# Block sums taken out of PSUM at the transposes, eps inside the sums of squares, and two gate tiles as a pair of seven half products

## The chip, the core and the metric

The kernel runs on one core of a Trainium2 chip. The core has a matrix engine (TensorE, PE in the profile; its weight loads are PEld), a vector engine (VectorE, DVE), a scalar engine (ScalarE, ACT), a general one (GpSimd, POOL), and a queue that only issues transfers (SyncE, SP). Each engine works through its own list of instructions in order, and engines wait for each other by semaphores. TensorE writes only to PSUM, eight banks of 128 x 512 float32; the other operands lie in SBUF. The metric is the device time of one execution in microseconds (us), less is better.

## What is computed

One decoder layer on x of 1024 tokens by 1024 channels, in float32:

```python
h = rms_norm(x, norm_w)                     # x * rsqrt(mean(x*x) + eps) * w, eps = 1e-5
proj = h @ w_in                             # 1024 x 7440
(a_q, a_k, a_v, a_gate, b_q, b_k, b_v, b_gate, b_low, m_a, m_b) = split(proj)
o_a = sliding_window_attention(rope(a_q), rope(a_k), a_v, sinks) * silu(a_gate)
log_a = log_sigmoid(b_low @ b_gate_up + bias) / 16
o_b = rms_norm(gated_linear_attention(b_q, b_k, b_v, log_a)) * silu(b_gate)
merged = sigmoid(m_a) * (o_a @ w_a_proj) + sigmoid(m_b) * (o_b @ w_b_proj)
return rms_norm(x + merged @ w_out, final_norm_w)
```

Attention has 16 query and 2 key heads of 64 with a window of 128; the linear attention has 4 heads with keys of 128 and values of 256. `m_a` and `m_b` are the two merge gates, 1024 columns each, that is eight tiles of 128 columns.

## The kernel before

**Products.** Every float32 operand of a large product is split into a high part (rounded to the type fp32r) and a low rest, and a product is three passes: high by high, high by low, low by high. `half_product` (L129) issues them for half of the 1024 channels: four slices of 128 channels, three matmuls each, of 128 x 128 weights by 512 tokens. `proj` (L137) joins two half products to one tile of 128 columns by 512 tokens.

**Token tiles.** At the start, eight tiles of 128 tokens are loaded and normalized by `token_tile` (L192). ScalarE squares a tile and sums it, GpSimd turns the sum into the reciprocal root by `rstd_of` (L144: mean plus eps, then power -0.5), VectorE multiplies by it and by the norm's weight `nwb`, which a transfer has copied to all partitions (L185, L198). TensorE transposes the tile into two PSUM banks, four blocks in each; ScalarE copies the high part out (L206) and VectorE subtracts for the low part (L207). These parts are `hT[th][i]`: `th` is the half of the tokens (tiles 0 to 3 or 4 to 7), `i` the half of the channels. The four blocks are called `b11`, `b21` (first tokens) and `b12`, `b22` (second tokens).

**Seven products.** Most columns of `w_in` are done two tiles at a time by `pair` (L567), which calls `seven_products` (L425): of the 2 x 2 blocks of weights and the 2 x 2 blocks of `hT` it makes seven half products instead of eight, as in Strassen's and Winograd's schemes. For this it needs four sums of blocks on the token side, `t1` to `t4`, each split into high and low. `t_sums` (L241) computes them from the split parts in SBUF: per slice of 128 channels ten sums on VectorE (L251, L252, L253, L258, L259), four copies on ScalarE (L245), four subtractions (L246). The order of the products in a pair is 1, 2 (with `b11`, `b21`), 6 (`t4`), 3 (`t2`), 5 (`t3`), 4 (`t1`), 7 (`b22`).

**Order of the stages.** First the token tiles; between them and behind them the first three tiles of the gate `m_a`, one half of the tokens at a time (`m_half`, L209). Then `t_sums`; the small product `low` (L329); tile 3 of `m_a` (`m_tiles([3])`, L348). Then the pairs: four of `m_b`, each followed by two calls of `log_gate`, with the rotary tables (`rotary_tables`, L353: some 30 small VectorE operations and two sines) behind the second; then pairs of `b_q`, `b_k`, `b_gate`, `b_v`. Then attention: in pass `i` of a loop `attend` (L717) works on one pair of heads while `prep` (L787) makes the queries and gates of the next. In the last pass there is nothing to prepare, and two tiles of `m_a` (4 and 5, from the list `fillers`) stand in its place. Then `gla(0)`, the linear attention of two heads, with tiles 6 and 7 of `m_a` spread over its steps by the list `pace`. Then the other two heads, with products of `w_a_proj` spread over them, and the merge, `w_out` and the final norm. There `finish` (L1075) sums four partial sums of squares, calls `rstd_of`, and scales and stores a token tile.

**What sets the order.** The program is written in one order, but a planner with a time line of its own puts each engine's instructions in line: where an engine would be free, it takes the earliest written instruction that it believes ready. Memory is taken from pools; a tile in a pool waits until the tiles that lay there before are released. The splits of weights (`split_w`, L116) run on ScalarE and on the engine in `rest[0]`, GpSimd at first.

Of the kernel before, what the change touches and what calls it, by code (L numbers as in the profile page):

```python
# [25 lines left out]
P = 128  # L26
# [43 lines left out]
def layer_kernel(ctx: ExitStack, tc: tile.TileContext, consts, x, positions, norm_w, w_in, a_sinks,  # L70
# [73 lines left out]
    def rstd_of(pool, ss, n, width):  # L144
        r = pool.tile([P, width], F32, name="rstd")
        nc.gpsimd.tensor_scalar(r, ss, 1.0 / n, EPS, ALU.mult, ALU.add)  # L146
        nc.gpsimd.tensor_tensor(r, r, mhalf[:, :width], ALU.pow)
        return r
# [21 lines left out]
    mhalf = const.tile([P, 8], F32, name="mhalf")  # L170
    nc.gpsimd.memset(mhalf, -0.5)
    c1 = ExitStack()
    c1.enter_context(banks(sc=2, pt=2, av=2))
    with ExitStack() as cx:
        xp = cx.enter_context(pool_of(name="xp", bufs=3, side="right"))
        xp1 = cx.enter_context(pool_of(name="xp1", bufs=1, side="right"))
        nwb = xp1.tile([P, D], F32, name="nwb")
        xts = [xp1.tile([P, D], F32, name=f"xt{t}") for t in range(NT)]

        def load(t):  # L180
            nc.sync.dma_start(xts[t], x[t * P : (t + 1) * P, :])
# [3 lines left out]
        nc.sync.dma_start(nwb, norm_w.to_broadcast([P, D]))  # L185
        load(1)
        w_first = [wtile(w_in, O_MA)]
        load(2)
        load(3)
        w_first.append(wtile(w_in, O_MA + P))  # L190

        def token_tile(t):  # L192
            xt = xts[t]
            junk = xp.tile([P, D], F32, name="junk", bufs=1)
            ss = xp.tile([P, 1], F32, name="ss")
            nc.scalar.activation(junk, xt, AF.Square, accum_out=ss)
            r = rstd_of(xp, ss, D, 1)
            nc.vector.scalar_tensor_tensor(xt, xt, r, nwb, ALU.mult, ALU.mult)  # L198
            for half in range(2):
                p = bank("sc" if half else "pt")  # L200
# [4 lines left out]
                hs, ls = (y[:, :, t % 4 * P : t % 4 * P + P] for y in hT[t // 4][half])  # L205
                nc.scalar.copy(hs, pv)  # L206
                nc.vector.tensor_sub(ls, pv, hs.bitcast(F32))  # L207

        def m_half(c, w, th, tag="pj"):  # L209
            p = bank(tag)  # L210
            for i in range(2):
                half_product(p, w[i], hT[th][i], i == 0, i == 1)
# [4 lines left out]
        for t in range(4):  # L217
            token_tile(t)
        for t in range(4, NT):
            load(t)  # L220
        w_first.append(wtile(w_in, O_MA + 2 * P))
        for t in range(4, NT):
            if t < 7:
                m_half(t - 4, w_first[t - 4], 0)
            token_tile(t)


    lp = gctx.enter_context(pool_of(name="lp", bufs=1, side="right"))
    rctx = ExitStack()
    rp = rctx.enter_context(pool_of(name="rp", bufs=1, side="right"))  # L230
    sctx = ExitStack()
    tp = sctx.enter_context(pool_of(name="tp", bufs=1))
# [913 lines left out]
```

## Time and profile before

| | us |
|---|---|
| median of 3 runs | 1078.42 (1078.25 to 1078.5) |
| the profiled execution | 1075.87 |
| its span, from first to last instruction | 1074.1 |
| TensorE busy | 1021.3 |
| VectorE busy | 766.1 |
| ScalarE busy | 544.8 |
| GpSimd busy | 520.4 |

The span is what the profile shows; the execution's own time is 1.8 us longer. A page of the profile gives busy times, the chain of work that ended last, and groups of instructions by the line that issued them. A row of such a group reads: line, engine, operation, output and input, shapes, how many; then busy time and the mean of one in ns; then the idle time of the engine before them and what ended it. A row of a time line has the start, the duration, the engine, the line and operation, and in brackets the idle time before it. The records of matmuls overlap, since TensorE begins one before the last has drained, so the time that a series of them takes is read from the starts.

### The profile page before, as it was taken

How to read it: one execution, taken by the hardware profiler on the slowest of the kernel's cores; microseconds unless marked ns; L12 is line 12 of the kernel's file. 1: busy time of each engine (PE TensorE's matmuls, PEld its weight loads, DVE VectorE, ACT ScalarE, POOL GpSimd, SP SyncE). 2: the span in 40 equal slices, each digit the busy share in tenths (PEclk: the TensorE clock that was granted, in tenths of full speed). 3: DMA queues.
4: the chain of work that ended last, by engine and by line, in shares of the span. 5: the costliest groups of instructions: out<-in, count | busy, mean ns of one | idle time of the engine just before them, and what ended most of it. 6: DMA issues, size and time to landing. Idle time of an engine off the chain costs nothing.

```text
span 1074.1 us, 16183 instructions
## 1 busy us (share of the span) xinstructions
PE 1021.3 (95%) x5544; PEld 867.9 (81%) x5544; DVE 766.1 (71%) x1318; ACT 544.8 (51%) x1320; POOL 520.4 (48%) x441
## 2 busy tenths in 40 slices
PE   4999999989999999999999999989999999997996
PEld 3786787867889998887888888878778887786996
DVE  5999877544765333369978887777856388899786
ACT  6345865333343123366766667647645244244455
POOL 6123555678897443755678676747843100000002
PEclk9999999989999999999999999999999999999999
DMA  8242444444233317221222222429775388443415
GB/s 264 72 135 69 138 147 139 155 138 135 102 110 108 117 40 216 60 60 55 74 60 60 79 70 79 137 85 297 245 224 159 109 274 256 131 145 99 158 60 196
DMA packets 126402, 141.06 MB, mean 131 GB/s; under 512 B 10352, under 2 KB 87024, under 8 KB 126320
## 3 DMA queue, kind: packets, MB, share of 16 engines
q1 hardware_dynamic: 126320, 140.03, 41.7%
q8 instruction: 44, 0.72, 0.3%
q14 instruction: 38, 0.31, 0.1%
HBM read 95.04 MB, written 40.24 MB: 126 GB/s over the span
## 4 chain that ended last, share of the span: by engine, by line
PE 55%; DVE 9%; POOL 5%; issue 4%; ACT 3%; DMA 2%; SPq 0%; POOLq 0%; DVEq 0%; ACTq 0%
PE pj L134 20%; PE sj L422 14%; PE sj L134 13%; PE av L773 2%; PE sc L733 2%; PE av L817 1%; DVE b L946 1%; DMA oraw<-sp_oa 1%; POOL q L651 1%; PE pt L757 1%; ACT sm L748 1%; POOL q L650 1%; PE sc L817 1%; DVE qb L714 1%; POOL cl L767 1%
## 5 line engine op out<-in xcount | busy, mean ns | idle before, releaser
L134 PE MATMUL pj<-o,wh 128*128 128x512 f32 x1088 | 354.5, 400 | 2.0 <-ACT o L206 1.9
L134 PEld LDWEIGHTS pj<-o,wh 128*128 128x128 f32 x1088 | 202.0, 190 | 43.7 <-ACT o L206 2.1
L134 PE MATMUL pj<-o,wl 128*128 128x512 f32 x544 | 216.4, 398 | 0.0
L118 POOL TENSOR_TENSOR wl<-sraw,wh 128x512 fp32r<-128x512 f32 (+1 forms) x98 | 157.8, 1627 | 110.4 <-ACT wh L117 105.3
L134 PEld LDWEIGHTS pj<-o,wl 128*128 128x128 f32 x544 | 102.8, 189 | 21.4
L134 PE MATMUL sj<-o,wh 128*128 128x512 f32 x352 | 111.1, 395 | 1.9 <-DVE o L459 1.0
L117 ACT CAST wh<-wr 128x1024 fp32r<-128x1024 f32 (+1 forms) x76 | 66.4, 890 | 77.6 <-PE sj L422 21.9
L146 POOL TENSOR_SCALAR rstd<-zs 128x1 f32<-128x1 f32 x8 | 2.7, 335 | 209.3 <-DVE zs L1078 208.8
L117 ACT CAST wh<-sraw 128x512 fp32r<-128x512 f32 (+1 forms) x98 | 63.4, 677 | 74.5 <-PE sj L134 20.8
L118 POOL TENSOR_TENSOR wl<-wr,wh 128x1024 fp32r<-128x1024 f32 x29 | 71.3, 2460 | 46.7 <-ACT wh L117 43.5
L134 PEld LDWEIGHTS sj<-o,wh 128*128 128x128 f32 x352 | 65.7, 187 | 18.4 <-ACT u L485 1.4
L476 DVE TENSOR_TENSOR u<-u,sj 128x512 f32<-128x512 f32 x48 | 32.9, 685 | 61.5 <-PE sj L422 32.7
L134 PE MATMUL sj<-o,wl 128*128 128x512 f32 x176 | 69.4, 394 | 0.0
L422 PE MATMUL sj<-wh,b 128*128 128x256 f32 x320 | 60.0, 289 | 7.0 <-DVE b L946 4.2
L422 PEld LDWEIGHTS sj<-wh,b 128*128 128x128 f32 x320 | 51.2, 197 | 7.7 <-DVE b L946 4.4
L422 PE MATMUL sj<-wh,o 128*128 128x256 f32 x320 | 55.8, 277 | 0.6 <-DVE o L539 0.6
L765 POOL TENSOR_TENSOR ch<-ph,cst 128x512 fp32r<-128x512 f32 x32 | 37.3, 1164 | 39.2 <-ACT ph L764 34.5
L748 ACT ACTIVATE sm<-sc,nm 128x129 f32<-128x129 f32 x128 | 45.7, 369 | 20.2 <-DVE nm L744 19.8
L134 PE MATMUL sj<-b,wh 128*128 128x512 f32 x160 | 49.2, 392 | 0.5 <-ACT wh L117 0.5
L459 DVE TENSOR_TENSOR c<-u,sj 128x512 f32<-128x512 f32 x48 | 32.7, 681 | 23.4 <-PE sj L422 6.4
L422 PEld LDWEIGHTS sj<-wh,o 128*128 128x128 f32 x320 | 48.7, 188 | 0.9 <-DVE o L539 0.8
L118 DVE TENSOR_TENSOR wl<-wr,wh 128x512 fp32r<-128x512 f32 (+1 forms) x47 | 41.6, 902 | 10.5 <-ACT wh L117 10.3
(313 smaller groups left out, 2706.7 us busy)
## 6 DMA issues: line engine op xcount, KB each, us to landing
sraw<-in_w_in_dram SPq DMA_DIRECT2D x32, 512.0 KB, 4.0
wr<-in_w_in_dram SPq DMA_DIRECT2D x26, 512.0 KB, 3.9
r<-sp_ob SPq DMA_DIRECT2D x28, 256.0 KB, 3.9
qs<-q SPq DMA_DIRECT2D x72, 64.0 KB, 2.0
xt<-in_x_dram SPq DMA_DIRECT2D x8, 512.0 KB, 8.5
sp_ma<-gt SPq DMA_DIRECT2D x16, 256.0 KB, 2.1
sp_mb<-c SPq DMA_DIRECT2D x16, 256.0 KB, 2.0
gt<-sp_cum SPq DMA_DIRECT2D x16, 256.0 KB, 3.5
```

Of the source, the lines that this page charges most:

```text
L117: nc.scalar.copy(h, raw)
L118: rest[0].tensor_sub(l, raw, h.bitcast(F32))
L134: nc.tensor.matmul(p, a[:, k, :], b[:, k, :], start=start and k == 0 and y == 0, skip_group_check=True, stop=stop and k == 3 and y == 2)
L422: nc.tensor.matmul(p, m[i][:, k, t * P : t * P + P], w[j][:, k, :], start=start and k == 0 and y == 0, skip_group_check=True, stop=stop an ...
L459: nc.vector.tensor_add(o, like(u[i][b], o), like(x[j][b], o))
L476: nc.vector.tensor_add(o[b], u[i][b], x[j][b])
L650: eng.tensor_mul(q, q, cos[:, sl])
L733: nc.tensor.matmul(s[:, h * 256 : h * 256 + 256], lq, kk[kv][x][:, k0 : k0 + 2, :].rearrange("p n t -> p (n t)"), start=x == 0, stop=x == 1)
L748: nc.scalar.activation(sm[:, j, :], sel[j // 2][:, j % 2, :], AF.Exp, bias=nm[:, j : j + 1], accum_out=den[:, j : j + 1])
L765: nc.gpsimd.tensor_mul(ch, ph.bitcast(F32), leb)
L773: nc.tensor.matmul(av[:, b * 256 : b * 256 + 256], val[:, blk, kv, :], part[:, 2 * b : 2 * b + 2, :], start=y == 0, stop=y == len(terms) - 1)
L817: nc.tensor.matmul(p, a[i], b[j], start=start and y == 0, stop=stop and y == 2)
```

## The change

1. **eps inside the sums of squares.** The token tiles get one more column that holds (eps x 1024)^0.5, and the squares are scaled by 1/1024, so that ScalarE's sum already is the mean plus eps. At the end the partial sums get a fifth column of eps. `rstd_of` becomes `power`, one GpSimd operation.
2. **The norm's weight** is loaded as one row; two matmuls with a row of ones bring it to all partitions, in two PSUM banks. The normalization becomes two operations per tile, one per half, each with its own transposes behind it.
3. **The block sums** are formed in `token_tile` for tiles 4 to 7, out of the PSUM banks of the transposes: six VectorE operations and one ScalarE copy per tile write the unsplit sums `tr`. Behind the first three gate tiles `t_split` splits them in the order `t4`, `t2`, `t3`, `t1`, with four copies and four subtractions each.
4. **Order of the start.** The first gate tile's first half is made in two parts of 256 tokens, the first after two token tiles (`m_part`). The splits of the first three weights run on VectorE. The rotary tables wait for the scan in the fourth `log_gate`.
5. **Gate tiles.** Tile 3 is no longer made at the start. Tiles 6 and 7 become a pair of seven products, behind the pairs of `m_b`. Tile 3 alone stands in the last pass of attention, tiles 4 and 5 in `gla(0)`.
6. **The end.** In `finish` the scaling of the last quarter goes from VectorE to GpSimd.

```diff
+    def power(pool, ss):
+        r = pool.tile([P, 1], F32, name="rstd")
+        nc.gpsimd.tensor_tensor(r, ss, mhalf, ALU.pow)
         return r
...
+        nwr = xp1.tile([1, D], F32, name="nwr")
+        ones = xp1.tile([1, P], F32, name="ones")
+        nc.vector.memset(ones, 1.0)
+        nc.scalar.activation(ones[:, :1], ones[:, :1], AF.Tanh)
+        nc.vector.memset(ones[:, :1], 1.0)
+        xts = [xp1.tile([P, D + 1], F32, name=f"xt{t}") for t in range(NT)]
+        for xt in xts:
+            nc.gpsimd.memset(xt[:, D:], (EPS * D) ** 0.5)
...
-        nc.sync.dma_start(nwb, norm_w.to_broadcast([P, D]))
+        nc.sync.dma_start(nwr, norm_w)
         load(1)
+        rest[0] = nc.vector
         w_first = [wtile(w_in, O_MA)]
         load(2)
         load(3)
-        w_first.append(wtile(w_in, O_MA + P))
+        nwb = [bank("av") for i in range(2)]
+        for i in range(2):
+            nc.tensor.matmul(nwb[i], ones, nwr[:, i * 512 : i * 512 + 512], start=True, stop=True)
...
-            nc.scalar.activation(junk, xt, AF.Square, accum_out=ss)
-            r = rstd_of(xp, ss, D, 1)
-            nc.vector.scalar_tensor_tensor(xt, xt, r, nwb, ALU.mult, ALU.mult)
+            nc.scalar.activation(junk, xt, AF.Square, scale=D**-0.5, accum_out=ss)
+            r = power(xp, ss)
             for half in range(2):
+                xh = xt[:, half * 512 : half * 512 + 512]
+                nc.vector.scalar_tensor_tensor(xh, xh, r, nwb[half], ALU.mult, ALU.mult)
                 p = bank("sc" if half else "pt")
...
+            if t >= 4:
+                r1, r2, r3, r4 = (y[:, :, sl] for y in tr)
+                (b11h, b11l), (b21h, b21l) = ([y[:, :, sl].bitcast(F32) for y in m] for m in hT[0])
+                nc.vector.tensor_sub(r1, ps[0], b11h)
+                nc.vector.tensor_sub(r1, r1, b11l)
+                nc.vector.tensor_sub(r2, ps[1], r1)
+                nc.scalar.copy(r3, ps[0])
+                nc.vector.tensor_sub(r3, ps[1], r3)
+                nc.vector.tensor_sub(r4, b21h, r2)
+                nc.vector.tensor_add(r4, r4, b21l)
...
+        token_tile(0)
+        token_tile(1)
+        p = bank("pj")
+        m_part(p, w_first[0], 0)
+        w_first.append(wtile(w_in, O_MA + P))
+        load(4)
+        w_first.append(wtile(w_in, O_MA + 2 * P))
+        for t in range(5, NT):
+            load(t)
+        rest[0] = nc.gpsimd
+        token_tile(2)
+        token_tile(3)
+        m_part(p, w_first[0], 1)
+        m_half(0, None, 0, p)
...
+    def t_split(i, tag):
+        m = [tph.tile([P, 4, 512], F32R, name=f"t{i}h"), slot(tpl if tag else tph, tag or "tl")]
+        r = tr[i - 1]
+        for k in range(4):
+            nc.scalar.copy(m[0][:, k, :], r[:, k, :])
+            nc.vector.tensor_sub(m[1][:, k, :], r[:, k, :], f(m, 0, k))
+        return m
...
-    fillers = list(range(4, 8))
+    fillers = [3, 4, 5]
...
-    t_sums()
+    t4, t2, t3, t1 = (t_split(*y) for y in ((4, None), (2, "t4"), (3, "t2"), (1, "t3")))
...
-    m_tiles([3])
...
         if c == 2:
-            rotary_tables()
+            with tc.issue_after(scan):
+                rotary_tables()
+    pair(O_MA + 6 * P, P, keep(sp_ma, 6 * P, "tanh"))
...
-                for _ in range(2):
-                    m_tiles([fillers.pop(0)])
+                m_tiles([fillers.pop(0)])
...
+    ssq = zw.tile([P, NT, 5], F32, name="ssq", bufs=1)
+    nc.gpsimd.memset(ssq[:, :, 4], EPS)
...
-        r = rstd_of(zw, ss, D, 1)
+        r = power(zw, ss)
...
-        nc.vector.tensor_scalar_mul(z1[:, o : o + 256], z1[:, o : o + 256], r)
+        nc.gpsimd.tensor_scalar_mul(z1[:, o : o + 256], z1[:, o : o + 256], r)
```

`m_part(p, w, q)` issues the same 24 products as `m_half`, but for 256 tokens each.

More of the change, by code (lines that the diff above doesn't have):

```diff
@@ L169, in layer_kernel @@
     le = cst[:, C_LE : C_LE + P]
[L170 removed]
+    mhalf = const.tile([P, 1], F32, name="mhalf")
     nc.gpsimd.memset(mhalf, -0.5)
+    sctx = ExitStack()
+    tpl = sctx.enter_context(pool_of(name="tpl", bufs=1))
+    sr = sctx.enter_context(pool_of(name="sr", bufs=4))
+    lp = gctx.enter_context(pool_of(name="lp", bufs=1, side="right"))
+    tctx = ExitStack()
+    td = tctx.enter_context(pool_of(name="td", bufs=1, side="right"))
+    tr = [slot(td if i == 1 else tpl, f"t{i}", F32) for i in range(1, 5)]
     c1 = ExitStack()
```

76 lines of the change are left out of this document (26 added, 50 removed).

## The prediction

> **What bounds the kernel now.** I read the page first: the share of each engine, then the chain that ended last, then tables of busy time by stretch for the start.
>
> ```profile
> PE 1021.3 (95%) x5544; PEld 867.9 (81%) x5544; DVE 766.1 (71%) x1318; ACT 544.8 (51%) x1320; POOL 520.4 (48%) x441
> ...
> PE 55%; DVE 9%; POOL 5%; issue 4%; ACT 3%; DMA 2%; SPq 0%; POOLq 0%; DVEq 0%; ACTq 0%
> ...
> 0.00:23.35 23.35, 8.56 (x37) 7.05 (x37) 11.86 (x13) 15.65 (x27) 13.04 (x20) 1.00 0.94 301
> 20.00:40.00 20.00, 19.33 (x88) 15.80 (x89) 19.29 (x36) 8.67 (x15) 8.81 (x9) 1.00 0.35 104
> 90.00:100.00 10.00, 7.80 (x33) 5.58 (x32) 9.73 (x13) 3.91 (x7) 2.99 (x2) 1.00 0.20 54
> 110.00:140.00 30.00, 29.05 (x126) 23.20 (x125) 25.77 (x33) 25.03 (x38) 17.11 (x12) 1.00 0.46 154
> 668.00:713.00 45.00, 44.10 (x246) 37.40 (x245) 37.22 (x72) 28.12 (x92) 31.15 (x28) 1.00 0.39 125
> 710.00:730.00 20.00, 16.72 (x103) 13.81 (x102) 10.90 (x38) 11.38 (x39) 9.94 (x15) 1.00 0.44 147
> ```
>
> TensorE (PE) is busy 95% of the span, so two things move the end: how many products there are, and where PE stands still. In a row of such a table stand the stretch, its length, then the busy time of PE, its weight loads, VectorE (DVE), ScalarE (ACT) and GpSimd (POOL), the granted clock and the DMA share. PE does 8.56 of the first 23.35 us, and waits again at 90 to 100 us while DVE is busy 9.73 of 10, and at 710 to 730. Next, the order of PE's work in the start.
>
> ```profile
> 23.35 1.20 PE L134 MATMUL pj<-o,wh 128*128 128x512 f32 x2
> ...
> 46.59 1.33 PE L134 MATMUL pj<-o,wh 128*128 128x512 f32 x3 [1.89 <-ACT o L206]
> ...
> 67.31 4.13 PE L332 MATMUL av<-o,lw 128*128 128x512 f32 x17
> 71.28 0.62 PE L134 MATMUL pj<-o,wh 128*128 128x512 f32 x2
> ...
> 82.70 0.62 PE L134 MATMUL sj<-o,wh 128*128 128x512 f32 x2
> ...
> 94.35 0.50 PE L134 MATMUL sj<-t4h,wh 128*128 128x512 f32 x1 [0.95 <-ACT t4h L245]
> 99.09 0.50 PE L134 MATMUL sj<-t2l,wh 128*128 128x512 f32 x1 [1.25 <-DVE t2l L246]
> 102.40 0.50 PE L134 MATMUL sj<-t4l,wh 128*128 128x512 f32 x1 [0.23 <-DVE t4l L246]
> ```
>
> The 17 products from 67.31 to 71.28 take 3.97 us: **0.233 us for a 512-column product**, though each record is longer, since products overlap. So an `m_half` (24 products) is 5.6 us, one gate tile with both halves 11.2 us, one product of a pair (12) 2.8 us, a pair (84) 19.6 us, the `low` product of one half 3.7 us. From 46.59 to 82.70 PE does three `m_half` of the second half (16.8), both `low` (7.5) and tile 3 (11.2); then the first pair starts, and waits 0.95 + 1.25 + 0.23 = 2.4 us for block sums.
>
> **The products.** Before, tiles 6 and 7 are 2 x 48 products; the pair needs 84. That is 96 - 84 = 12 fewer, 2.8 us of PE. But work also moves: tile 3 (11.2) leaves the start, the pair (19.6) enters the stage of pairs, and after the last `attend` stands one tile instead of two (11.2 less); `gla(0)` keeps two. The pairs' stage is PE's, so **+19.6 us** there in full; its seven splits of 128x512 on GpSimd (2.35 us is the row of a 128x1024 one, below) replace two of 128x1024, some 5 us more in a stage where GpSimd is busy 17.11 of 30 us; its loads (two of 512 KB) and four stores are those that two tiles have. Its 11 DVE operations of 0.6 us lie under 19.6 us of PE.
>
> **The start.** DVE decides when PE gets the second half.
>
> ```profile
> 16.29 0.68 DVE L207 TENSOR_TENSOR o<-pt,o 128x512 fp32r<-128x512 f32 x1
> 16.89 0.68 DVE L207 TENSOR_TENSOR o<-sc,o 128x512 fp32r<-128x512 f32 x1
> 17.49 2.97 DVE L198 SCALAR_TENSOR_TENSOR xt<-xt,rstd,nwb 128x1024 f32<-128x1024 f32 x1
> ...
> 17.03 2.35 POOL L118 TENSOR_TENSOR wl<-wr,wh 128x1024 fp32r<-128x1024 f32 x1
> ...
> L198 DVE SCALAR_TENSOR_TENSOR xt<-xt,rstd,nwb 128x1024 f32<-128x1024 f32 x8 | 14.1, 1760 | 10.7 <-DMA nwb<-in_norm_w_dram 6.3 <-POOL rstd L147 4.2
> L251 DVE TENSOR_TENSOR tr<-o,o 128x512 f32<-128x512 f32 x8 | 8.6, 1084 | 0.1
> L258 DVE TENSOR_TENSOR tr<-o,tr 128x512 f32<-128x512 f32 x8 | 7.5, 961 | 0.0
> L252 DVE TENSOR_TENSOR tr<-o,o 128x512 f32<-128x512 f32 x8 | 6.9, 868 | 0.1
> L259 DVE TENSOR_TENSOR tr<-tr,o 128x512 f32<-128x512 f32 x8 | 6.4, 820 | 0.0
> L253 DVE TENSOR_TENSOR tr<-tr,tr 128x512 f32<-128x512 f32 x8 | 6.4, 806 | 0.0
> ...
> 31.64 0.34 DVE L356 TENSOR_SCALAR ang<-ang,cst 128x256 f32<-128x256 f32 x1
> ...
> 44.03 0.29 DVE L389 TENSOR_SCALAR rad<-rad 128x256 f32<-128x256 f32 x1
> ...
> 48.77 0.69 DVE L207 TENSOR_TENSOR o<-sc,o 128x512 fp32r<-128x512 f32 x1 [0.81 <-ACT o L206]
> ```
>
> Operations of 512 columns follow each other every 0.60 us (16.29, 16.89, 17.49). A product with the norm weight that runs beside GpSimd's split takes 2.97 us instead of 1.28. The forty sums L251 to L259 cost 35.8 us. The change leaves 24 (six for each of tiles 4 to 7, 14.4 us). The rotary operations between 31.64 and 44.3 (about 11 us without three L207) go behind the scan of the second pair, into the stretch 110 to 140, where DVE works 25.77 of 30 us and ACT 25.03; Sin brings its table loads there too. It fits by spreading over the next pairs, the gate pair without a log gate among them; I count nothing, and 2 us if PE has to wait for it. Splits of the first weights go to DVE: three of about 1.2 us (two operations of 0.6), taking away GpSimd's 2.35.
>
> Count to the last L207, from about 6 us on (the first square ends at 5.5 in before): norm products 16 x 0.6 = 9.6, L207 16 x 0.6 = 9.6, sums of tiles 4 to 6 10.8, weight splits 3.6, small operations 2, waits for x and first latencies 2: 37.6. **Second half ready at 44 us** against 46.59. PE then needs 16.8 + 3.7, and the first pair starts at 64.5 to 68.2, by whether the first `low` fits in PE's wait before 44; its bank frees only when tile 7's norm products have read the broadcast weight. Middle 66.4: 16.3 earlier than 82.70. The sums are then ready: splits (16 x 0.6) and last sums end near 60, the first is wanted at 72, so the 2.4 us go as well. Start: **-18.7 us**; ends -21 and -12.
>
> The weight's broadcast on PE has no row of its own: 512 columns of f32 in four transposes of 0.9 us, or 2.0 us in eight records of the nearest plain f32 product:
>
> ```profile
> 8.47 1.11 PE L203 MATMUL pt<-cst,xt 128*128 128x128 f32 x4 [8.47 <-DVE xt L198]
> ...
> L856 PE MATMUL av<-bq,bk 128*128 128x64 f32 x8 | 1.3, 248 | 0.0
> ```
>
> So 1.8 to 4 us for both, I take 3.4. PE idles until 8.47 in before, and the weight's 512 KB load held DVE until 7.13. I count it nothing; without the cover it is 1 us. The quarter products of the first tile (256 columns) fall in PE's early gaps. Tanh early, the eps column and its eight memsets lie before the first load lands. On SP the third weight's load waits for its buffer until the first split is done, with the loads of tiles 5 to 7 behind it in the written order; that is near 12 us, and those tiles are wanted after 20, so nothing.
>
> The row of 2.97 us fits the Trainium skill, SBUF — State Buffer, "Who interferes with whom": a DVE operation with two SBUF inputs is blocked by a GpSimd operation reading SBUF, one with an input in PSUM isn't. By it the new norm products are never stretched; without it they would cost 2 us more. The tail's scaling on GpSimd meets the same rule from the other side.
>
> **The end of attention.**
>
> ```profile
> 600.00:631.50 31.50, 31.50 (x175) 26.98 (x175) 25.92 (x52) 20.98 (x71) 22.46 (x17) 1.00 0.24 68
> ...
> 714.24 2.80 PE pj L134 x12
> ```
>
> A pass of the loop over head pairs takes 31.5 us, PE full, DVE at 82%; 714.24 is a piece of the chain of waits. In the last pass, without 11.2 us of filler, PE could save all 11.2, but DVE can only close its gaps: 37.22 of 45 us from 668 to 713 is 83%; at 95% the stretch is 39. I take **-5 us** of the 11.2 (ends -1 and -10); the rest becomes idle PE.
>
> **The tail.** Per token tile GpSimd loses a scaling of 0.49 and takes the 128x256 product from DVE:
>
> ```profile
> 1067.89 0.49 POOL L146 TENSOR_SCALAR rstd<-zs 128x1 f32<-128x1 f32 x1
> ...
> 1069.44 0.35 DVE L1085 TENSOR_SCALAR o<-o,rstd 128x256 f32<-128x256 f32 x1
> ...
> L593 POOL TENSOR_SCALAR c<-c,bnw 128x512 f32<-128x512 f32 x16 | 28.3, 1770 | 6.9 <-DVE c L592 3.6 <-issue 2.6 <-POOL wl L118 0.7
> ```
>
> Half of 1.57 to 1.77 is 0.8 on GpSimd against 0.35. Behind it waits the next tile's power, and ScalarE and DVE wait for that. -0.5 +0.5: **0**, ends -0.6 and +0.8.
>
> **Sum.** +19.6 - 18.7 - 5 + 0 = -4.1. The profiled execution took 1075.87 (span 1074.1): 1071.8. The runs shown have a median of 1078.42, 2.5 more; on that scale **1074.3 us**.
>
> **Rivals.** *More is gained*: DVE closes all its gaps at the end of attention (-10) and the start reaches -20: 1078.4 + 19.6 - 30 = 1068. For it: PE is full in 44.10 of the 45 us, so the filler does stand in DVE's way. Against: DVE is at 83% even so. Chance 0.13.
>
> *Nothing comes back at the end of attention*: DVE, ScalarE and GpSimd latencies set the pace, -1 there: 1078.3, same. For it: 710 to 730 already has 3.3 us of idle PE, and of PE's filler only the 2.80 us at 714.24 is a long piece of the chain there. Chance 0.12.
>
> *PE restarts at a lower clock*. In before a stretch with waits had a granted clock of 0.83, and its products were longer:
>
> ```profile
> 780.00:790.00 10.00, 8.38 (x37) 6.72 (x38) 5.23 (x16) 5.88 (x18) 4.77 (x8) 0.83 0.86 282
> ...
> L134 PE MATMUL pj<-o,wh 128*128 128x512 f32 x13 | 5.4, 502 | 0.0
> ```
>
> That stretch loses 0.17 x 10 = 1.7 us. The change makes PE wait some 6 us before 44 and again after attention; twice 1.7 gives 1077.7, same. Chance 0.08. The Trainium skill, TensorE: Matmul & The Clock Gate, "What's actually happening", says that an idle window of about 3.4 us halves the clock for as long again; the waits of before were all shorter than that, so the start here can't confirm it.
>
> *Slower: DVE becomes the bound of the start.* If the planner puts all sums ahead of tile 7's L207, or the banks the sums hold delay the next tile's transposes, the second half comes at 53 instead of 44, with nothing else to fill PE: 1074.3 + 9 = 1083. It is slower than before from 50.3 us on. For it: DVE is already busy 19.29 of the 20 us from 20 to 40. Against: 11 us of rotary work leave just there. Chance 0.25.
>
> **Chances.** The forecast as such 0.42. Faster by over 0.2% (2.2 us, about what a measurement of this kernel can tell from no change): 0.42 + 0.13 = 0.55; within: 0.12 + 0.08 = 0.20; slower: 0.25. The forecast alone spans 1070 to 1076; with both outer cases the range is 1067 to 1083.
>
> **What would show it.** The first `sj` product at 64 to 69 us and no wait for t sums there; the second half's first product near 44; PE idle 5 to 7 us more between 680 and 730; the stage of pairs 19 to 20 us longer; the tail from the last product unchanged. It is wrong if the first `sj` product comes after 72, or if the time from the last pair to `gla` doesn't shrink.

## The result, and the profile after

| | before | after |
|---|---|---|
| median | 1078.46 us (1078.25 to 1080.88) | 1091.01 us (1089.49 to 1092.15) |
| ratio, 95% interval | | 1.0109 (1.0086 to 1.0131) |
| span of the profiled execution | 1074.1 us | 1090.3 us |

The change makes the kernel 1.1% slower; the forecast was 1074.3, its range ended at 1083. The page's busy times and the shares of the chain that ended last, after:

```profile
PE 1031.5 (95%) x5560; PEld 874.5 (80%) x5560; DVE 758.0 (70%) x1318; ACT 546.4 (50%) x1330; POOL 514.5 (47%) x444
...
PE 58%; DVE 10%; POOL 4%; ACT 3%; issue 3%; DMA 2%; SPq 0%; POOLq 0%; ACTq 0%; DVEq 0%
```

TensorE is busy 10.2 us longer, though the pair needs 12 products less. That already hints at products that run slower. To find where the 16.2 us of span come from, I cut the span at four stores that every version has. The rows are those of the tile view (how many, shortest, median and longest in ns, then first and last start in us); for before:

```profile
L606 SPq DMA_DIRECT2D sp_mb<-c x16: 319/320/456, 104.3 to 174.2; - x16
...
L603 SPq DMA_DIRECT2D sp_bv<-c x16: 359/363/533, 342.0 to 411.2; - x16
...
L785 SPq DMA_DIRECT2D sp_oa<-oa x16: 319/332/526, 493.2 to 721.2; - x16
...
L893 SPq DMA_DIRECT2D sp_ob<-bg x8: 370/384/533, 748.9 to 861.8; - x8
```

And after:

```profile
L638 SPq DMA_DIRECT2D sp_mb<-c x16: 319/320/384, 79.7 to 163.4; - x16
...
L635 SPq DMA_DIRECT2D sp_bv<-c x16: 359/362/864, 350.4 to 421.1; - x16
...
L819 SPq DMA_DIRECT2D sp_oa<-oa x16: 319/341/643, 501.7 to 735.3; - x16
...
L927 SPq DMA_DIRECT2D sp_ob<-bg x8: 370/384/533, 762.5 to 875.0; - x8
```

The last start of each row ends a stage; differences of neighbours give its length:

| stage, us | before | after | difference | predicted |
|---|---|---|---|---|
| start and pairs of `m_b`, to the last `sp_mb` | 174.2 | 163.4 | -10.8 | -18.7 |
| other pairs, to the last `sp_bv` | 237.0 | 257.7 | +20.7 | +19.6 |
| attention, to the last `sp_oa` | 310.0 | 314.2 | +4.2 | -5 |
| `gla`, to the last `sp_ob` | 140.6 | 139.7 | -0.9 | 0 |
| merge, `w_out`, norm, to the end of the span | 212.3 | 215.3 | +3.0 | 0 |

So the pair costs about what was predicted. The start gives 8 us less than predicted and attention takes 9 us more: these two are most of the miss. The prediction's own sign of being wrong, that the time from the last pair to `gla` doesn't shrink, is there. Busy times by stretch, after; PE is full in the third row and stands still for a part of the others:

```profile
20.00:40.00 20.00, 18.42 (x109) 15.38 (x107) 19.75 (x34) 10.02 (x20) 1.10 (x3) 1.00 0.74 211
60.00:80.00 20.00, 16.43 (x70) 12.79 (x69) 13.40 (x19) 10.78 (x17) 7.55 (x6) 1.00 0.13 39
110.00:140.00 30.00, 30.00 (x132) 24.45 (x131) 26.32 (x45) 20.23 (x33) 12.66 (x9) 1.00 0.40 133
150.00:170.00 20.00, 15.41 (x55) 11.44 (x54) 14.53 (x26) 13.91 (x22) 8.10 (x8) 0.85 0.35 111
710.00:730.00 20.00, 12.57 (x49) 10.28 (x50) 15.45 (x32) 5.38 (x17) 7.27 (x7) 0.51 0.12 40
```

The last row begins 8.8 us behind the second store of the next-to-last pass of attention (701.24, shown below). In before the same place is at 698.40:

```profile
698.40:718.40 20.00, 18.56 (x103) 15.21 (x101) 14.11 (x33) 7.67 (x22) 9.55 (x8) 1.00 0.28 92
```

There TensorE issues 49 products where before issued 103, and the granted clock is 0.51 where it was 1.00. The waits of PE in the start, in its time line:

```profile
42.92 0.50 PE L134 MATMUL pj<-o,wh 128*128 128x512 f32 x1 [2.05 <-DVE o L230]
...
69.18 0.50 PE L582 MATMUL pj<-low,gu 128*128 128x512 f32 x1 [2.31 <-DVE low L367]
69.52 0.63 PE L134 MATMUL sj<-o,wh 128*128 128x512 f32 x2
...
73.73 0.70 PE L134 MATMUL sj<-o,wh 128*128 128x512 f32 x2 [1.25 <-DVE low L367]
```

The second half is ready at 42.92 (44 was predicted), the first `sj` product comes at 69.52 instead of 82.70, and nothing waits for a block sum. But `low` is late: its low part is split by VectorE (L367), which stands behind the splits of `t` in the written order, and PE loses 2.31 and 1.25 us.

In the last pass of attention the four longest waits of PE for ScalarE and VectorE are 9.4 us together (same view):

```profile
708.94 0.38 PE L807 MATMUL av<-ph,vv 128*128 128x256 f32 x1 [2.02 <-ACT ph L798]
713.09 1.11 PE L791 MATMUL pt<-cst,sm 128*128 128x128 f32 x4 [3.76 <-DVE pl L800]
717.79 0.55 PE L807 MATMUL av<-ph,vv 128*128 128x256 f32 x1 [2.10 <-DVE fo L817]
720.52 0.47 PE L791 MATMUL pt<-cst,sm 128*128 128x128 f32 x1 [1.51 <-ACT sm L788]
```

And VectorE does other work between attention's own operations, here the splits of q for `gla(0)`. The second `pl` of the pass, the low part of attention's transposed weights, for which PE waits 3.76 us, stands behind the three casts:

```profile
708.74 3.35 DVE L844 CAST qh<-bq 128x512 fp32r<-128x512 f32 x3
...
712.36 0.68 DVE L800 TENSOR_TENSOR pl<-pt,ph 128x512 fp32r<-128x512 f32 x1
...
713.61 3.24 DVE L845 TENSOR_TENSOR ql<-bq,qh 128x512 fp32r<-128x512 f32 x3
```

In before the same splits stand in this pass too, but the second `pl` stands ahead of them:

```profile
697.35 0.69 DVE L766 TENSOR_TENSOR pl<-pt,ph 128x512 fp32r<-128x512 f32 x1 [2.28 <-ACT ph L764]
697.96 3.50 DVE L811 CAST qh<-bq 128x512 fp32r<-128x512 f32 x3
...
702.37 1.88 DVE L812 TENSOR_TENSOR ql<-bq,qh 128x512 fp32r<-128x512 f32 x3
```

So with one tile in the pass instead of two the planner's order on VectorE is another one: `pl` comes 11.1 us behind the store at 701.24, in before 7.7 us behind the one at 689.64.

The length of this pass I take from the second store of the pass before it to the last store of `sp_oa`. Its beginning in the time line of SP, before:

```profile
689.64 0.32 SPq L785 DMA_DIRECT2D sp_oa<-oa  x1
```

and after:

```profile
701.24 0.64 SPq L819 DMA_DIRECT2D sp_oa<-oa  x1
```

That is 721.2 - 689.64 = 31.6 us before and 735.3 - 701.24 = 34.1 after, with 11.2 us of products less. At that point after is 11.6 us late, against 9.9 at the last `sp_bv`: 1.7 us are lost in the passes before, 2.5 in the last.

### The profile page after: what moved, and what is told of

Its sections match the earlier page's. It is cut to its first block, busy times and chain, and to the rows that moved or that the text cites. A ratio compares the mean times of both kernels' runs of the same rounds, so it can differ in the third digit from the quotient of the medians.

```text
span 1090.3 us, 16253 instructions
## 1 busy us (share of the span) xinstructions
PE 1031.5 (95%) x5560; PEld 874.5 (80%) x5560; DVE 758.0 (70%) x1318; ACT 546.4 (50%) x1330; POOL 514.5 (47%) x444
## 4 chain that ended last, share of the span: by engine, by line
PE 58%; DVE 10%; POOL 4%; ACT 3%; issue 3%; DMA 2%; SPq 0%; POOLq 0%; ACTq 0%; DVEq 0%
PE pj L134 21%; PE sj L134 15%; PE sj L453 13%; PE sc L767 2%; PE av L807 2%; PE av L850 1%; PE pt L791 1%; DMA oraw<-sp_oa 1%; DVE sm L790 1%; DVE qb L748 1%; DVE b L980 1%; DMA qs<-q 1%; DVE qa L747 1%; PE av L890 1%; PE sc L850 1%
## 5 line engine op out<-in xcount | busy, mean ns | idle before, releaser
L134 PE MATMUL pj<-o,wh 128*128 128x512 f32 x1008 | 328.9, 400 | 2.5 <-DVE o L230 2.0
L118 POOL TENSOR_TENSOR wl<-sraw,wh 128x512 fp32r<-128x512 f32 (+1 forms) x105 | 162.6, 1566 | 152.3 <-ACT wh L117 148.1
L134 PEld LDWEIGHTS pj<-o,wh 128*128 128x128 f32 x1008 | 187.3, 191 | 40.3 <-DVE o L230 2.5
L134 PE MATMUL pj<-o,wl 128*128 128x512 f32 x504 | 200.2, 398 | 0.0
L134 PE MATMUL sj<-o,wh 128*128 128x512 f32 x376 | 119.8, 398 | 2.1 <-DVE low L367 1.3
L117 ACT CAST wh<-sraw 128x512 fp32r<-128x512 f32 (+1 forms) x105 | 67.4, 673 | 88.2 <-PE sj L134 25.5
L134 PEld LDWEIGHTS pj<-o,wl 128*128 128x128 f32 x504 | 95.3, 189 | 19.7
L117 ACT CAST wh<-wr 128x1024 fp32r<-128x1024 f32 (+1 forms) x74 | 64.3, 885 | 77.0 <-PE sj L453 20.7
L134 PEld LDWEIGHTS sj<-o,wh 128*128 128x128 f32 x376 | 71.0, 190 | 20.3 <-issue 1.7
L118 POOL TENSOR_TENSOR wl<-wr,wh 128x1024 fp32r<-128x1024 f32 x24 | 58.8, 2450 | 34.5 <-ACT wh L117 34.5
L134 PE MATMUL sj<-o,wl 128*128 128x512 f32 x188 | 74.8, 398 | 0.0
L134 PE MATMUL sj<-t,wh 128*128 128x512 f32 x156 | 62.6, 402 | 0.0
L118 DVE TENSOR_TENSOR wl<-wr,wh 128x512 fp32r<-128x512 f32 (+1 forms) x50 | 45.3, 923 | 13.5 <-ACT wh L117 13.4
## 6 DMA issues: line engine op xcount, KB each, us to landing
r<-sp_ob SPq DMA_DIRECT2D x28, 256.0 KB, 4.1
sp_mb<-c SPq DMA_DIRECT2D x16, 256.0 KB, 2.0
gt<-sp_cum SPq DMA_DIRECT2D x16, 256.0 KB, 3.7
sp_bg<-c SPq DMA_DIRECT2D x16, 256.0 KB, 2.1
```

The lines of the kernel that those rows point to most:

```text
L117: nc.scalar.copy(h, raw)
L118: rest[0].tensor_sub(l, raw, h.bitcast(F32))
L134: nc.tensor.matmul(p, a[:, k, :], b[:, k, :], start=start and k == 0 and y == 0, skip_group_check=True, stop=stop and k == 3 and y == 2)
```

## The experiments

Each kernel was timed beside the kernel before on the same chip; spans of stages come from the one profiled execution of each. Executions of one kernel differ: those of e2 took 1072.57 to 1082.63 us. Stages with the same code show how much of that reaches the table: the start of after, e3, e4, e6, e7, e9 and e13 takes 163.1 to 164.3, the other pairs take 255.6 to 257.7 with the gate pair and 237.0 to 239.2 without it, and the rest takes 212.0 to 215.3 in the kernels that share its code with after. A smaller difference between two rows says nothing by itself. Times of stages in the order of the table above, with the number of gate tiles (11.2 us of products each) in the start, the last pass and `gla(0)`:

| kernel | tiles start / pass / gla | to `sp_mb` | pairs | attention | `gla` | rest | median us | ratio, interval |
|---|---|---|---|---|---|---|---|---|
| before | 1 / 2 / 2 | 174.2 | 237.0 | 310.0 | 140.6 | 212.3 | | |
| after | 0 / 1 / 2, pair | 163.4 | 257.7 | 314.2 | 139.7 | 215.3 | 1091.01 | 1.0109 (1.0086 to 1.0131) |
| e1 | 0 / 1 / 2, pair | 170.8 | 256.3 | 311.1 | 139.6 | 213.4 | 1095.28 | 1.0149 (1.0123 to 1.0174) |
| e2 | 1 / 2 / 2 | 174.0 | 238.3 | 309.2 | 140.6 | 212.5 | 1077.22 | 0.9986 (0.9966 to 1.0006) |
| e3 | 0 / 2 / 3 | 163.7 | 239.0 | 311.2 | 154.1 | 213.2 | 1086.71 | 1.0079 (1.0050 to 1.0108) |
| e4 | 0 / 2 / 1, pair | 164.3 | 256.0 | 314.4 | 133.9 | 213.1 | 1084.43 | 1.0059 (1.0032 to 1.0085) |
| e5 | 1 / 2 / 2 | 166.9 | 239.0 | 310.8 | 138.8 | 214.3 | 1071.94 | 0.9928 (0.9905 to 0.9952) |
| e6 | 0 / 1 / 2, pair | 163.4 | 255.6 | 309.1 | 145.9 | 212.0 | 1088.18 | 1.0089 (1.0058 to 1.0120) |
| e7 | 0 / 3 / 2 | 163.5 | 239.2 | 312.0 | 155.4 | 214.9 | 1084.21 | 1.0033 (0.9992 to 1.0074) |
| e8 | 1 / 2 / 2 | 166.2 | 237.3 | 311.2 | 139.5 | 212.6 | 1071.55 | 0.9926 (0.9907 to 0.9944) |
| e9 | 0 / 0 / 3, pair | 163.3 | 256.5 | 304.9 | 157.7 | 213.5 | 1096.95 | 1.0170 (1.0129 to 1.0210) |
| e10 | 0 / 1 / 2, pair | 165.4 | 257.1 | 313.7 | 140.4 | 214.3 | 1092.28 | 1.0120 (1.0096 to 1.0145) |
| e12 | 0 / 2 / 1, pair | 165.4 | 256.0 | 312.5 | 136.2 | 211.9 | 1084.41 | 1.0042 (1.0021 to 1.0063) |
| e13 | 0 / 2 / 2, pair | 163.1 | 256.7 | 312.5 | 139.1 | 212.0 | 1086.18 | 1.0056 (1.0034 to 1.0077) |

**e1 and e2: the two halves of the change.** e1 is the kernel before with the moves of the gate tiles alone; e2 is the changed kernel with the gate tiles where they were, that is without these edits. e1, against before:

```diff
-    fillers = list(range(4, 8))
+    fillers = [3, 4, 5]
...
-    m_tiles([3])
...
+    pair(O_MA + 6 * P, P, keep(sp_ma, 6 * P, "tanh"))
...
-                for _ in range(2):
-                    m_tiles([fillers.pop(0)])
+                m_tiles([fillers.pop(0)])
```

> The kernel before with only the gate tiles moved (tiles 6 and 7 a pair of seven products, tile 3 alone in the last pass of attention, 4 and 5 in gla(0), none of it at the start); sums, eps and start as before. Theory 'cover': gate tiles in the last pass of attention and in gla(0) cost nearly nothing, since DVE, ScalarE and latencies set the pace there, so the pair brings +19.6 us into a stage where PE is the bound, the start gives back 11.2 at most (less, as the old block sums on DVE are late already), and the last pass gives back nothing: 1086 to 1096 us. Rival 'start': the loss comes from the new token tiles and rotary placement; then this kernel stays at 1074 to 1081.

> The changed kernel with the gate tiles where they were before (tile 3 at the start, 4 and 5 in the last pass, 6 and 7 in gla(0), no gate pair); all other parts of the change stay. Theory 'cover': the new start is a gain of about 2 us up to the first pair and 2.4 us of waits for block sums: 1071 to 1077 us. Rival 'start': the new start costs, 1082 us or more.

e1 took 1095.28: the moves alone cost 1.5%, as the theory of the missing cover had it. e2 took 1077.22, no difference that can be measured. It has the first `sj` product at 78.87, 3.8 us ahead of before, and has lost it again by the last `sp_mb` (174.0 against 174.2). So the new start alone brought nothing, and the loss lies with the tiles.

**e3 and e4: which place is dear.** e3 drops the pair and puts the extra tiles into `gla(0)`; e4 keeps the pair and takes a tile out of `gla(0)` into the last pass. e3, against the changed kernel:

```diff
-    fillers = [3, 4, 5]
+    fillers = list(range(3, 8))
...
-    pair(O_MA + 6 * P, P, keep(sp_ma, 6 * P, "tanh"))
...
+                for _ in range(2):
-                m_tiles([fillers.pop(0)])
+                    m_tiles([fillers.pop(0)])
```

And e4, against the changed kernel:

```diff
+                for _ in range(2):
-                m_tiles([fillers.pop(0)])
+                    m_tiles([fillers.pop(0)])
```

> The changed kernel without the gate pair: tiles 3 and 4 in the last pass of attention, 5, 6 and 7 in gla(0). Theory 'cover': the 19.6 us of the pair go away, the last pass gets its cover back (-2.5), and a third tile in gla(0) costs 0 to 8 us because that stretch is not PE's: 1065 to 1077 us, under both kernels. Rival: PE is the bound there as elsewhere, the two tiles cost their 22.4 us again: 1088 to 1092.

> The changed kernel, with tiles 3 and 4 in the last pass of attention as two tiles stood there before, and only tile 5 in gla(0). Theory 'cover': the last pass is back at its old length and TensorE's clock stays up there, so 2 to 6 us less than the changed kernel, 1085 to 1089, though gla(0) has one tile less. Rival: moving a tile within PE-bound work changes nothing, 1090 to 1092.

e3 missed: 1086.71. Without the pair the other pairs take 239.0 instead of 257.7, so the pair costs **18.7 us**. But the third tile in `gla(0)` takes 13.5 us more (154.1 against 140.6 in e2), more than its products. The kernel gives a reason: behind `gla(0)`, `pace` holds the tiles' products, in groups of three, each for the step `min(15, 2 + i // 2)`. So group 26 and all behind it wait for step 15, the last; with two tiles that is 6 groups of 32, with three 22 of 48, or 15.4 us of products. In e3's trace 63 products of gate tiles stand together from 761 to 777, where PE is busy for all of the 16 us. Another `pace` was not tried. e4 went the expected way, 1084.43, 6.6 below after, yet not where I expected it: attention is as long with two tiles as with one (314.4 against 314.2), and the gain is in `gla`, which is 5.8 shorter:

```profile
L928 SPq DMA_DIRECT2D sp_ob<-bg x8: 359/370/1047, 763.0 to 868.6; - x8
```

The second tile of the last pass, which the change took away, was free there.

**e5 and e10: the rotary tables.** In e5 they are free again to stand where the planner puts them, in e2; e10 does the same to the changed kernel. The edit of both:

```diff
-            with tc.issue_after(scan):
-                rotary_tables()
+            rotary_tables()
```

> The kernel of e2 (new start, gate tiles as before) with the rotary tables free to stand where the planner puts them, as before, and not behind the scan. Theory 'rotary in the pairs costs': the 3.6 us that e2 wins at the first sj product (78.87 against 82.70) and has lost again by the last sp_mb store (174.0 against 174.2) go to the rotary work that stands there; without it the last sp_mb store comes at 170 to 172 and the end 2 to 4 us before e2's: 1073 to 1075. Rival 'GpSimd's and ScalarE's weight splits cost there whatever stands beside them': last sp_mb store at 173.5 to 174.5 and 1076 to 1079. Rival 'rotary work goes back into the start and holds up the second half': first sj product after 80, last sp_mb store at 174 or later.

> The changed kernel with one part undone: the rotary tables free to stand where the planner puts them. Theory 'the move of the rotary work costs' as between e2 and e5 (last sp_mb store 7.1 us earlier): last sp_mb store at 156 to 159 in place of 163.4, total 1084 to 1087. Rival 'without tile 3 in the start the rotary work has no cover there either': first sj product 2 to 6 us later than 69.52, last sp_mb store at 161 to 164, total 1088 to 1092.

e5 took **1071.94, 0.72% below before**, and the last `sp_mb` comes at 166.9, even earlier than expected. Two stretches, first of e2:

```profile
60.00:80.00 20.00, 20.00 (x87) 16.17 (x86) 13.73 (x18) 5.19 (x10) 5.05 (x4) 1.00 0.14 48
130.00:150.00 20.00, 18.89 (x81) 14.80 (x80) 19.90 (x37) 11.38 (x17) 6.70 (x5) 1.00 0.42 145
```

then of e5:

```profile
60.00:80.00 20.00, 18.13 (x76) 14.27 (x75) 19.72 (x37) 8.11 (x11) 2.48 (x2) 0.98 0.13 43
130.00:150.00 20.00, 20.00 (x89) 16.33 (x88) 12.12 (x20) 13.87 (x23) 6.00 (x6) 1.00 0.49 163
```

VectorE is full where the rotary work is: from 130 to 150 in e2, where PE needs it for its pairs and the next weights' sums, and from 60 to 80 in e5, where PE has the products of the first gate tiles, `low` and tile 3, which don't need it. e10 went to the rival, and to a little beyond its number: 1092.28, not measurably different from after. Its first `sj` product comes at 71.38, 1.9 us later than after's. There tile 3 isn't in the start, and PE runs out (windows of e10):

```profile
60.00:80.00 20.00, 11.77 (x39) 8.62 (x38) 19.73 (x31) 5.34 (x9) 4.48 (x3) 0.83 0.13 39
```

The first `log_gate` waits 5.33 us for a split of `low` (its product starts at 70.79). The time line of VectorE shows the last split of `low` at 78.78, behind the splits of `t`, and that of PE the second product of the pair, which by the profile waits for it:

```profile
76.05 2.50 DVE L295 TENSOR_TENSOR t<-t,t1h 128x512 fp32r<-128x512 f32 x4
...
78.78 0.68 DVE L367 TENSOR_TENSOR low<-av,low 32x512 fp32r<-32x512 f32 x1
...
79.61 0.86 PE L134 MATMUL sj<-o,wh 128*128 128x512 f32 x2 [2.90 <-DVE low L367]
```

So tile 3 and the rotary work pay for each other. By the last `sp_mb`: with both in the start 166.9 (e5), with the tile alone 174.0 (e2), with the rotary work alone 165.4 (e10), with neither 163.4 (after). Taking tile 3 away is worth 10.6 us if VectorE has nothing else to do there, and 1.5 if it has.

**e6, e7, e9, e13: what the last pass is made of.** e6 splits q for `gla` on ScalarE and GpSimd (in `gla(0)` alone); e7 is e2 with tile 3 as a third tile of the last pass; e9 is after with no tile there; e13 makes the tile there twice.

e6, against the changed kernel:

```diff
-        return qT, kT, kp, split(bpe, "q", qT, 512, nc.vector.tensor_copy, nc.vector.tensor_sub), bg
+        early = hd < 2
+        ops = (nc.scalar.copy, nc.gpsimd.tensor_sub) if early else (nc.vector.tensor_copy, nc.vector.tensor_sub)
+        return qT, kT, kp, split(bpe, "q", qT, 512, *ops), bg
```

e7, against e2:

```diff
-    fillers = list(range(4, 8))
+    fillers = list(range(3, 8))
...
-    m_tiles([3])
...
-                for _ in range(2):
+                for _ in range(3):
```

e9, against the changed kernel:

```diff
-            else:
-                m_tiles([fillers.pop(0)])
```

e13, against the changed kernel:

```diff
             else:
+                m_tiles([fillers[0]])
                 m_tiles([fillers.pop(0)])
```

> The changed kernel with the q splits of gla(0) on ScalarE and GpSimd in place of DVE. Theory 'foreign work on DVE lengthens the last pass' (the three casts at 708.74 and three subtractions at 713.61 stand among attend's row maxima and pl parts): the last sp_oa store comes 3 to 6 us before the changed kernel's 735.3, total 1085 to 1088. Rival 'the chain of latencies itself is the floor': last sp_oa store within 1 us of 735, total 1089 to 1092. Rival 'the half clock is the price': only if PE's waits there fall below 2 us does the clock stay at 1.00; then -1 to -2.

> The kernel of e2 with tile 3 taken from the start into the last pass of attention, which then has three tiles (3, 4, 5) and gla(0) two; no pair. Theory 'the last pass has a floor near 31 us set by attend's own chain, into which two tiles fit': the third tile fills the 2.5 to 3 us that PE still waits there and costs the rest of its 11.2: the time from the store of pass 6's second half to the last store grows from 31.4 to 39 to 41 us; the start gains 9 to 10, total 1074 to 1078. Rival 'still free': 31 to 33 us, total 1067 to 1070. Rival 'it costs in full': 42.6, total 1077 to 1080.

> The changed kernel without its tile in the last pass: all three tiles (3, 4, 5) in gla(0). Theory 'floor': the time from the store of pass 6's second half to the last store, 34.1 us with one tile and 32.9 with two, stays at 32 to 36; gla(0) grows by 12 to 14, total 1100 to 1106. Rival 'PE-bound, one tile is worth 11.2 there': 23 to 25 us, total 1091 to 1094.

> The changed kernel with its gate tile of the last pass made twice there (same result, 48 products or 11.2 us of PE more; gla(0) keeps two tiles). Theory 'PE's waits in the last pass halve its clock, and filler prevents that': in the changed kernel PE waits 2.02, 3.76 and 2.10 us there and runs 20.48 us at half clock; with the tile twice the waits come late, the half clock is 3.4 us or none, the time from the store of pass 6's second half to the last store falls from 34.1 to 31.5 to 33 us and the total is no longer than before the doubling: 1088 to 1092. Rival 'PE's work counts there': 11.2 us more, 42 to 45 us for that pass, 1100 to 1103. Rival 'half': 1094 to 1098.

The length of the last pass, taken as above, with the granted clock in it:

| tiles there | kernel | last pass, us | clock |
|---|---|---|---|
| 0 | e9 | 26.5 | 0.74 |
| 1 | e6, q's splits off VectorE | 29.5 | 0.77 |
| 1 | after, e1, e10 | 34.1, 33.7, 34.2 | 0.70 |
| 2 | before, e2, e3 | 31.6, 31.4, 31.4 | 1.00 |
| 2 | e4, e13, e5, e8, e12 | 32.9, 32.9, 33.0, 33.0, 32.9 | 0.95 |
| 3 | e7 | 32.0 | 1.00 |

Between the two stores TensorE issues 12 products of gate tiles in e9 (those of `gla(0)` count too), 28 in after, 77 in e5 and 114 in e7: between the first and the last lie 23.8 us of products and 5.5 us of time, and one tile is the longest. Only with three tiles is PE full in the pass (32.0 us in e7; in after 23.6 of 34.0). Nor is the pass a fixed floor: e9 missed both its theories (26.5, neither 32 to 36 nor 23 to 25). In e13, with 48 products more, whose result is the same, the kernel is *faster*, 1086.18 against 1091.01, with intervals that don't overlap (1088 to 1092 was expected). Two rows of its windows answer to the row of 710 to 730 above:

```profile
699.00:720.00 21.00, 20.28 (x109) 16.98 (x107) 16.70 (x35) 12.31 (x41) 10.37 (x10) 1.00 0.22 73
720.00:732.60 12.60, 9.99 (x52) 8.16 (x52) 6.16 (x23) 4.68 (x18) 5.12 (x5) 0.86 0.26 85
```

In the changed kernel the trace's record of the clock has one stretch of 20.48 us at half speed in the last pass; in e13, as in e4, it has one of 3.41. The pass of e13 is 1.1 us shorter instead of 11.2 longer. But e13 doesn't show that the clock is the reason, since the order on VectorE changed with it: the second `pl` stands ahead of q's casts in before, e13 and every kernel with two or three tiles there, and behind them in after, e1 and e10. What the half clock costs shows in the kernels with two tiles, which all have the same order: where the record has no stretch at half speed in the pass it takes 31.4 to 31.6, where it has one of 3.41 us 32.9 to 33.0, so such a stretch goes with some 1.5 us. The spans of after and e13 differ by 6.9; beside the 1.1 us, 1.9 lie ahead of that pass, 0.6 in `gla` and 3.3 in the merge and `w_out`, where both have the same instructions. Those I don't ascribe to the tile; what is shown is that its products cost nothing there.

e6 shows what q's splits cost there. With them off VectorE the second `pl` comes 8.0 us behind the store instead of 11.1, and the pass takes 29.5, 4.6 less. The last `sp_oa` comes 7.2 us before after's (728.1 against 735.3), more than the expected 3 to 6; the other 2.6 lie ahead of the pass. But `gla` then takes 145.9 instead of 139.7 and gives it back; the total of 1088.18 can't be told from after's. Whether the subtractions on GpSimd (1.37 us in the median) or the clock (6.83 us at half speed there) lengthen `gla` was not tried.

e7's pass has the 32 us of the rival 'still free', and the third tile is all but done by its end: ScalarE reads the last of the six half tiles at 715.79, 1.1 us behind the last `sp_oa`. But the tile stands where others have the first operations of `gla(0)`: VectorE's first copies of `att` come at 715.76, behind the pass, in e2 at 712.66, 8.9 us ahead of its end. So the first `sp_ob` comes 34.4 us after the last `sp_oa` (749.1 - 714.7), in e2 27.7. `gla` then takes 155.4. Its total of 1084.21 is above all three forecasts: a tile out of the start (-10.5) and into the last pass (+2.8) and `gla` (+14.8) loses 7.

**e8: the tail.** e5 with the last scaling back on VectorE.

```diff
 e8, against e5
-        nc.gpsimd.tensor_scalar_mul(z1[:, o : o + 256], z1[:, o : o + 256], r)
+        nc.vector.tensor_scalar_mul(z1[:, o : o + 256], z1[:, o : o + 256], r)
```

> The kernel of e5 with the tail's 128x256 scaling back on DVE (the squares still carry eps, so GpSimd has the power alone). Theory 'the scaling on GpSimd lengthens the tail' (it took 1.03 us there against 0.35 on DVE, and the DVE product beside it 0.57 against 0.48): from the last product on PE to the issue of the last store 5 to 5.5 us in place of 6.7, total 1.0 to 1.7 us below e5's: 1070 to 1071. Rival 'the tail hangs on the DMA or on ScalarE': 6.4 to 7 us, total as e5, 1071.5 to 1073.

The end of after, in the time line: the last product, the last scaling, the issue of the last store.

```profile
1079.69 0.28 PE L453 MATMUL sj<-wl,o 128*128 128x256 f32 x1
...
1085.14 1.22 POOL L1121 TENSOR_SCALAR o<-o,rstd 128x256 f32<-128x256 f32 x1
...
1086.39 0.33 SPq L1122 DMA_DIRECT2D out_dram<-o  x1
```

and of e8:

```profile
1057.77 0.28 PE L454 MATMUL sj<-wl,o 128*128 128x256 f32 x1
...
1061.40 0.34 DVE L1121 TENSOR_SCALAR o<-o,rstd 128x256 f32<-128x256 f32 x1
...
1062.93 0.59 SPq L1122 DMA_DIRECT2D out_dram<-o  x1
```

From the last product to the last issue 6.7 us after (6.7 in e5 too), 5.2 in e8, as the theory had it. The median is only 0.4 below e5's, within the spread; the trace shows the step, the total doesn't.

**e12: the pair at its best.** Rotary free, two tiles in the last pass, one in `gla(0)`, the tail on VectorE, the pair kept: e4 with the edits of e10 and e8.

> The changed kernel with what the runs so far say is cheaper: rotary tables free, two gate tiles in the last pass and one in gla(0), the tail's scaling on DVE; the pair of seven half products stays. Theory 'the pair itself loses': against e8 it saves tile 3 in the start (9 to 10) and a tile in gla(0) (5) and costs 18.4: 3 to 5 us above e8, 1074 to 1076, so no faster than 0.5% below before. Rival 'once the order is right the pair pays by its 12 products': at or below e8, 1067 to 1071.

1084.41, a miss: it is 12.9 us above e8, not 3 to 5. The stages say why: against e8 the other pairs take 18.7 more; the start gives 0.8 back instead of the 9 to 10 I had taken from e2 and e3 (e10 shows the reason), and `gla` 3.3 instead of 5. (With one tile left in `gla(0)` the clock stands at half there for 20.48 us in e12 and for 13.65 in e4.) The best version found is **e8, 1071.55 us, 0.74% below before** (interval 0.9907 to 0.9944), with e5 the same within the spread: the change's new start and eps, without its pair and with the rotary work left free.

## Why the prediction was wrong

**The pair, +19.6: right.** 239.0 to 257.7 (e3 to after), and 237.3 to 256.0 (e8 to e12): 18.7 both times, and 20.7 from before to after.

**The end of attention, -5: the step that failed most**, by 9.2 us. "I take -5 us of the 11.2 (ends -1 and -10)" was worked out from DVE's share in a stretch of 45 us, as if PE and DVE shared the work and one would close its gaps when the other had less. The runs show a chain of latencies between PE, ScalarE and VectorE with gaps that the filler fills: taking one of two tiles away gives nothing (after against e4), and removing the filler lets PE wait 2 to 4 us at a time. What made the pass longer, 34.1 against 31.6, goes with two things. With less of PE's work in it the planner put q's casts ahead of the second `pl`, where before had them behind it, and PE waits 3.76 us for that `pl`; without q's splits on VectorE the pass takes 4.6 less (e6). And the clock fell to half for 20.48 us; what that cost by itself stays open, since no run changed the clock and left the order. Only an empty pass is shorter by 5 us (26.5 in e9 against 31.6 before), and then the tiles cost more in `gla`. The 1.7 us that were lost in the passes before stay open.

**The start, -18.7: the second failed step**, by 7.9 us. Its first term, -16.3 to the first `sj` product, came out as -13.2, since "the first pair starts at 64.5 to 68.2" counted products of `low` but not VectorE's splits of it, for which the first `log_gate` waits. Its second term, 2.4 us of waits for sums that go, is right in itself, but waits for `low` came instead, 2.31 us ahead of the first `sj` product and 1.25 behind it. The rest went in the pairs of `m_b`: after needs 93.9 us from the first `sj` to the last `sp_mb` (163.4 - 69.52), before 91.5. Late in these pairs, at 162.29, PE waits 2.36 us for the high part of a weight (L117, ScalarE); before has no wait from 116 us to its last `sp_mb`. The term "I count nothing" for the rotary work was wrong by up to 7.1 us (e2 against e5, with tile 3 in the start); with tile 3 gone it is no loss (e10). And the -18.7 gave the new start a gain of its own beside tile 3's 11.2: with the rotary work moved it has none (e2: -0.2); left free it has 7.3 (e5), and then tile 3's removal has only 1.5. I had added two gains that can't both be had.

**`gla(0)`, nothing said.** The prediction noted that it keeps two tiles and looked no further. A tile there costs 3 to 6 us from one to two (e12 against e8, e4 against after) and 13 to 18 from two to three (e3, e9), the latter with `pace` as it is. Taking the pair's tile from there instead of from the last pass loses less (e4, 1084.43), but 3 to 6 us don't pay for 18.7 either.

**The tail, 0, ends -0.6 and +0.8: +1.5.** From the last product to the last issue before took 5.2 us (1065.01 to 1070.21), after 6.7. The scaling on GpSimd takes 1.03 us in the mean, 8.1 us for eight, and not the 0.8 taken as half of a 512-column row, and VectorE's product beside it 0.57 instead of 0.48:

```profile
L1121 POOL TENSOR_SCALAR o<-o,rstd 128x256 f32<-128x256 f32 x8 | 8.1, 1026 | 0.2
...
L1119 DVE SCALAR_TENSOR_TENSOR o<-o,rstd,fnw 128x256 f32<-128x256 f32 x8 | 4.6, 570 | 2.6 <-POOL rstd L146 2.5
```

The same group before:

```profile
L1083 DVE SCALAR_TENSOR_TENSOR o<-o,rstd,fnw 128x256 f32<-128x256 f32 x8 | 3.9, 483 | 1.5 <-POOL rstd L147 1.4
```

The next tile's power waits behind the scaling, so VectorE's wait for it grows from 1.4 to 2.5 us. The other 1.5 us of the last stage lie in the merge and `w_out`. With the same code there the stage takes 212.0 in e13 and 215.3 in after, so I leave it open.

**The rivals.** "Nothing comes back at the end of attention" was right as far as it went, and too mild. "PE restarts at a lower clock" came true in the last pass, with 20.48 us of half clock instead of a stretch of 10 us at 0.83, but its price beside the new order is not known. Its remark that the waits of before were all shorter than 3.4 us overlooks the first, of 8.47 us, which its own line shows. "DVE becomes the bound of the start" didn't happen at the place named (the second half came at 42.92), but DVE did set the start by `low`, and in e10 openly. None had the cost of a filler that is taken from where it was free.

## What to carry to other kernels

A filler has the price of the place it stands in, not of its products: here 11.2 us of products cost between nothing and 18 us, and the kernel with a tile made twice was faster than with the tile once. Taking a filler out also changes what a planner puts next on the other engines, so look at their order before and after. Before work is moved, measure each place with a tile more and a tile less; two moves that use the same cover (tile 3 and the rotary work) must be priced together. A scheme that saves an eighth of the products still loses if, for it, products leave gaps in which they cost nothing and enter a stage in which TensorE is full.

## What the hardware showed that was not expected

In the last pass of the changed kernel the clock fell to half at 710.3, in the second of three waits of 2.02, 3.76 and 2.10 us (they end at 708.94, 713.09 and 717.79), and stayed there for 20.48 us, to 730.8. PE was busy again for most of that: from 720 to 730 for 8.75 us of 10, and from 723.43 on without a wait.

```profile
720.00:730.00 10.00, 8.75 (x35) 7.17 (x36) 5.51 (x17) 2.04 (x5) 2.14 (x2) 0.50 0.07 27
...
723.43:730.78 7.35, 7.35 (x28) 6.02 (x29) 3.73 (x11) 0.35 (x1) 2.14 (x2) 0.50 0.00 1
```

The clock also fell for 6.83 us at 164.2, where the two nearest waits are only 2.36 and 2.04 us long (they end at 162.29 and 165.07). The stretches at half speed that lie inside the traces are all multiples of 3.41 us: 3.41, 6.83, 10.24, 13.65, 20.48. The Trainium skill, TensorE: Matmul & The Clock Gate, "What's actually happening", has the window of about 3.4 us and says that one sustained busy window brings the clock back. The length of the window agrees with these multiples. But here the clock stayed down for six of them, the last two of them with PE busy throughout; which work counts as busy is not shown.
